# First sums of the up phase, their low parts and the norm steps rearranged in a Strassen feed-forward kernel

## The chip, the cores and the metric

The kernel runs on one core of one Trainium2 chip. The metric is the device time of one execution in microseconds (us); smaller is better. The core has a matrix engine (PE, TensorE), a vector engine (DVE, VectorE), a scalar engine (ACT, ScalarE), a general engine (POOL, GpSimd) and a queue (SP, SyncE) that here only starts transfers. POOL can start transfers too, and those can add what they carry to what stands at the destination ("accumulating transfer").

## The reference

One inference step of one encoder layer: 16 meta tokens and 1024 new frames of one stream, and 32 frames of a running stream, 1072 tokens of 1024 channels in all. A convolution group and an attention group run side by side; the change lies behind them, in the feed-forward part and the last norm:

```python
def rmsnorm(x, g):
    xf = x.astype(jnp.float32)
    r = lax.rsqrt(jnp.mean(xf * xf, axis=-1, keepdims=True) + EPS)
    return (xf * r).astype(x.dtype) * g

def conv_ffn(x, gate_past, g, w_up, dw_w, dw_b, w_down):
    h = rmsnorm(x, g)
    u = h @ w_up                                   # 1024 -> 2 x 2816
    gate, up = u[..., :D_FF], u[..., D_FF:]
    gate_ext = jnp.concatenate([gate_past, gate], axis=1)
    y = jax.nn.silu(depthwise_causal_conv(gate_ext, dw_w, dw_b)) * up   # width 3
    return x + y @ w_down, gate_ext[:, -(FFN_CONV_WIDTH - 1):]
...
    y_prompt = rmsnorm(xp, norm_final)[:, N_META:]
```

## The kernel before, in words

Channels lie on the 128 partitions, tokens along the rows. Every float32 product is made from three matmuls of a rounded format: each operand is split into a high part (a cast on ACT) and a low part (original minus high part), and the products high·high, high·low and low·high are summed (`mm3`). So each operand costs one cast and one subtraction. `hilo(hi, lo, raw)` does both, the subtraction on DVE or, with a fourth argument, on POOL (lines 1143 to 1145).

The feed-forward part is in two phases. **Up phase:** the 2816 channels are 22 blocks `f` of 128, each with a gate row `G` and an up row `Y`. Blocks 0 and 1 are multiplied plainly, in 16 groups of 24 matmuls (`group(f, u, p, c)`), blocks 2 to 21 by Strassen's method with 7 products instead of 8 (`up_strassen`). The activations' side of Strassen needs four sums of the four quarters b11, b12, b21, b22 of the input, times the norm's gain `g2`: b12-b11, b22-(b12-b11), b22-b12 and b21-(b22-(b12-b11)). These are the "first sums". `t_stage(p)` makes them for the two token halves `p`, in four steps `j` each, while PE works on the 16 plain groups: ACT scales the four quarters into `hraw`, DVE makes three sums into `traw` and the fourth into `t4`, ACT casts `traw` into the high parts `THI` and DVE subtracts for the low parts `TLO` (lines 1220 to 1236). The plain groups' weights go through two pairs of buffers (`plain`): `w_plain(1, 1)` overwrites the pair that block 0 used for `u` = 1. `rms2` gives the last third of the tokens its norm factors: sums by PE, a power on POOL, small steps on DVE, a diagonal on ACT, and a broadcast by PE (`last_rms`, lines 245 to 264). `gate_done` and `y_done` make a block's gate: multiply by the norm, convolution of width 3, silu, product.

**Down phase:** block rows come back from memory through three row buffers (`rb`, `gx`, `rbg`): `Feed.fill` issues a load on SP, `Feed.take` splits what has landed with `hilo` and frees the buffer for the next load. First 24 groups of plain products (`d_mm` over `arow`, line 1527), then eight Strassen steps (`STEPS`) whose results DVE adds to the residual rows `X` (line 1337), then the last four blocks plainly with the final norm (`rms_steps`, `final`). While the 24 groups run, `y_done(21)` stores the last block's row from the memory that the results of the last eight groups are copied to. `xd_add` adds the saved residual to `X` by accumulating transfers on POOL.

A scheduler decides the order on each engine where the program does not: PE's order is that of the program, ACT, DVE, POOL and SP are ordered by estimated readiness and priority, and each engine then runs its list strictly in order. Buffers are guarded by semaphores: whoever writes a buffer waits for its last reader.

Of the kernel before, what the change touches and what calls it, by code (L numbers as in the profile page):

```python
# [60 lines left out]
FS = 1  # L61
# [95 lines left out]
def body(nc, tc, cp, wp, xp, dp, io):  # L157
# [966 lines left out]
    traw = new(pr, "traw", 3 * PNS[0])  # L1124
    hraw = [new(pr, f"hraw{i}", 4 * PNS[0]) for i in range(2)]
# [3 lines left out]
    with tc.tile_pool(name="psB", bufs=1, space=PSUM, reuse_waits="tile") as pf:  # L1129
# [13 lines left out]
        def hilo(hi, lo, raw, eng=None):  # L1143
            nc.scalar.copy(hi, raw)  # L1144
            return (eng or nc.vector).tensor_tensor(out=lo, in0=raw, in1=hi.bitcast(F32), op=ALU.subtract)  # L1145
# [14 lines left out]

        def w_plain(f, u, hi, lo):
            raw = wraw(up_src(f, u))
            hilo(hi, lo, raw)
            ups[f, u] = kv(hi), kv(lo)
# [55 lines left out]
        def t_stage(p):  # L1220
            n = PNS[p]
            tt_ = nc.vector.tensor_tensor
            t4 = t4s[p][:, 0:4 * n].rearrange("p (a b) -> p a b", a=4)
            tr = traw[:, 0:3 * n].rearrange("p (a b) -> p a b", a=3)
# [146 lines left out]
        for i in range(4):  # L1371
            group(0, 0, i // 2, i % 2)
            if 0 < i < 3:
                next(last_rms)
            next(t0s)
        w_plain(1, 0, *plain[:2])
        for i in range(4):
            group(0, 1, i // 2, i % 2)
            if i == 1:
                next(last_rms)  # L1380
                gate_done(0)
            if i % 2:
# [36 lines left out]
        class Feed:  # L1419
# [59 lines left out]
        GQ = ((5, 1), (2, 0), (7, 1), (4, 0))  # L1479
# [230 lines left out]
```

## Time and profile before

| | |
|---|---|
| median of three runs | 1084.97 us (1083.0 to 1085.17) |
| the profiled execution | 1084.88 us |
| its span, first to last instruction | 1083.1 us |
| PE busy | 1046.9 us (97%) |
| DVE busy | 874.4 us (81%) |
| ACT busy | 499.5 us (46%) |
| POOL busy | 180.7 us (17%) |
| mean granted TensorE clock | 0.992 of full speed |

The profile is one execution. Times in it are us from the span's start. "PE 97% busy" is an average over stages, and a busy PE is not one at its peak, since matmuls overlap. What counts is where PE stands still, what ended that, and at which granted clock it goes on (1.00 is 2.4 GHz, 0.50 is 1.2 GHz). A time written as `a <-b` is idle time of an engine that ended when b was done.

### The profile page before, as it was taken

How to read it: one execution, taken by the hardware profiler on the slowest of the kernel's cores; microseconds unless marked ns; L12 is line 12 of the kernel's file. 1: busy time of each engine (PE TensorE's matmuls, PEld its weight loads, DVE VectorE, ACT ScalarE, POOL GpSimd, SP SyncE). 2: the span in 40 equal slices, each digit the busy share in tenths (PEclk: the TensorE clock that was granted, in tenths of full speed). 3: DMA queues.
4: the chain of work that ended last, by engine and by line, in shares of the span. 5: the costliest groups of instructions: out<-in, count | busy, mean ns of one | idle time of the engine just before them, and what ended most of it. 6: DMA issues, size and time to landing. Idle time of an engine off the chain costs nothing.

```text
span 1083.1 us, 19942 instructions
## 1 busy us (share of the span) xinstructions
PE 1046.9 (97%) x7741; PEld 1016.4 (94%) x7741; DVE 874.4 (81%) x1616; ACT 499.5 (46%) x1072; POOL 180.7 (17%) x199
## 2 busy tenths in 40 slices
PE   8999999989999989999999999999998999999995
PEld 7999997758999989999999999999998899999995
DVE  7799999999887788878888888888869766975645
ACT  8532226997776844333333433433336513522332
POOL 1112000002335121001001001000103330210042
PEclk9999999999999989999999999999999999999998
DMA  8344332124953122243242243233245794832214
GB/s 265 81 105 98 87 87 52 39 54 74 171 137 118 51 75 87 69 140 90 70 137 91 71 126 103 70 119 109 70 126 168 237 200 81 254 106 75 60 31 131
DMA packets 68119, 116.82 MB, mean 108 GB/s; under 512 B 11312, under 2 KB 44328, under 8 KB 68024
## 3 DMA queue, kind: packets, MB, share of 16 engines
q1 hardware_dynamic: 58200, 97.44, 28.7%
q0 software_dynamic: 9536, 17.89, 9.8%
q8 instruction: 61, 1.00, 0.4%
q14 instruction: 34, 0.28, 0.1%
q10 hardware_dynamic: 288, 0.22, 0.1%
HBM read 78.90 MB, written 27.51 MB: 98 GB/s over the span
## 4 chain that ended last, share of the span: by engine, by line
PE 55%; DVE 6%; DMA 3%; ACT 3%; issue 2%; POOL 1%; POOLq 0%; DVEq 0%; SPq 0%; ACTq 0%
PE mm L1209 49%; PE mm L241 2%; PE mm L239 2%; PE mm L240 2%; DMA raw<-wdn 1%; DVE bl L1145 1%; DMA gx<-yq 1%; DVE tl L1145 1%; DVE x L1262 1%; ACT hraw L1229 1%; DVE sl L1145 1%; DMA yd<-x 1%; DVE x L1582 1%; DVE gx L1256 0%; DVE wlo L1145 0%
## 5 line engine op out<-in xcount | busy, mean ns | idle before, releaser
L1209 PE MATMUL mm<-bh,sl 128*128 128x264 f32 (+1 forms) x912 | 214.7, 285 | 1.0 <-DVE x L1337 1.0
L365 DVE SCALAR_TENSOR_TENSOR acc<-glu,prm,acc 128x1090 f32<-128x1090 f32 (+3 forms) x180 | 168.0, 967 | 0.4
L1209 PEld LDWEIGHTS mm<-bh,sl 128*128 128x128 f32 x912 | 157.6, 189 | 1.2 <-DVE x L1337 1.2
L1209 PE MATMUL mm<-th,rawr 128*128 128x266 f32 (+1 forms) x640 | 121.3, 285 | 0.0
L1209 PE MATMUL mm<-bl,sl 128*128 128x264 f32 (+1 forms) x424 | 120.9, 285 | 0.0
L1209 PE MATMUL mm<-bh,wlo 128*128 128x264 f32 (+1 forms) x440 | 118.0, 285 | 0.0
L1209 PE MATMUL mm<-bh,whi 128*128 128x264 f32 (+1 forms) x440 | 113.1, 285 | 3.1 <-DVE x L1337 3.1
L1337 DVE TENSOR_TENSOR x<-x,mm 128x264 f32<-128x264 f32 (+7 forms) x238 | 75.8, 346 | 47.9 <-PE mm L1209 47.8
L239 PE MATMUL mm<-hi,whi 128*128 128x352 f32 (+3 forms) x312 | 104.8, 336 | 0.1
L240 PE MATMUL mm<-lo,whi 128*128 128x352 f32 (+3 forms) x312 | 102.3, 328 | 1.7 <-DVE lo L275 1.7
L241 PE MATMUL mm<-hi,wlo 128*128 128x352 f32 (+3 forms) x312 | 101.7, 326 | 0.0
L1209 PEld LDWEIGHTS mm<-th,rawr 128*128 128x128 f32 x640 | 101.2, 189 | 0.0
L1209 PE MATMUL mm<-th,sl 128*128 128x264 f32 (+1 forms) x352 | 93.1, 285 | 0.2 <-ACT th L1144 0.2
L1209 PE MATMUL mm<-tl,rawr 128*128 128x266 f32 (+1 forms) x320 | 91.4, 286 | 0.0
L1209 PEld LDWEIGHTS mm<-bh,whi 128*128 128x128 f32 x440 | 79.0, 189 | 3.5 <-issue 2.3
L1209 PEld LDWEIGHTS mm<-bh,wlo 128*128 128x128 f32 x440 | 80.7, 189 | 0.0
L1209 PEld LDWEIGHTS mm<-bl,sl 128*128 128x128 f32 x424 | 80.0, 189 | 0.0
L1209 PE MATMUL mm<-bl,whi 128*128 128x264 f32 (+1 forms) x272 | 77.4, 285 | 0.0
L1144 ACT CAST sl<-x 128x512 fp32r<-128x512 f32 (+1 forms) x41 | 29.7, 726 | 76.0 <-PE mm L1209 40.8
L1209 PEld LDWEIGHTS mm<-th,sl 128*128 128x128 f32 x352 | 64.2, 189 | 0.5 <-ACT th L1144 0.4
L240 PEld LDWEIGHTS mm<-lo,whi 128*128 128x128 f32 x312 | 59.2, 190 | 3.4 <-DVE lo L275 3.1
L239 PEld LDWEIGHTS mm<-hi,whi 128*128 128x128 f32 x312 | 59.1, 189 | 1.6 <-DVE acc L365 0.6
(350 smaller groups left out, 2941.0 us busy)
## 6 DMA issues: line engine op xcount, KB each, us to landing
x<-wup SPq DMA_DIRECT2D x40, 256.0 KB, 2.7
x<-wup SPq DMA_DIRECT2D x20, 512.0 KB, 4.3
yq<-x SPq DMA_DIRECT2D x32, 264.0 KB, 3.1
wlo<-raw POOLq DMA_DIRECT2D x16, 512.0 KB, 4.5
raw<-win SPq DMA_DIRECT2D x12, 512.0 KB, 3.5
raw<-wdn SPq DMA_DIRECT2D x12, 512.0 KB, 3.7
rb<-yq SPq DMA_DIRECT2D x10, 528.0 KB, 5.0
yq<-gx SPq DMA_DIRECT2D x16, 264.0 KB, 4.7
```

The source lines that it names most:

```text
L239: nc.tensor.matmul(ps, whi(k), xhi(k), start=first and i == 0, stop=False)
L240: nc.tensor.matmul(ps, whi(k), xlo(k), start=False, stop=False)
L241: nc.tensor.matmul(ps, wlo(k), xhi(k), start=False, stop=last and i == n - 1)
L365: nc.vector.scalar_tensor_tensor(out=a, in0=e[:, a0 + k:a1 + k], scalar=pcol("cw", p * CW + k), in1=a, op0=ALU.mult, op1=ALU.add)
L1144: nc.scalar.copy(hi, raw)
L1145: return (eng or nc.vector).tensor_tensor(out=lo, in0=raw, in1=hi.bitcast(F32), op=ALU.subtract)
L1209: nc.tensor.matmul(ps, w[:, j, :], x[:, j, :], start=first and j + i == 0, stop=j == 3 and i == 2, skip_group_check=True)
L1229: nc.scalar.activation(h[:, 2 * i * n + lo_:2 * i * n + hi_], src, AF.Copy, scale=pcol("g2", k))
L1262: nc.vector.scalar_tensor_tensor(out=Tm[:, NMETA:], in0=G[:, NMETA + k:k + GOW], scalar=pcol("fw", f * FW + k), in1=Tm[:, NMETA:], op0=ALU ...
L1337: nc.vector.tensor_tensor(out=z, in0=z, in1=banks[k][:, lo_:hi_], op=ALU.add)
L1582: nc.vector.scalar_tensor_tensor(out=x, in0=x, scalar=pcol("g3", k), in1=R[:, lo_:hi_], op0=ALU.mult, op1=ALU.mult)
```

## The change

There are four edits.

1. `t_stage` scales only one quarter (b11) on ACT; DVE takes the other three from `X` and applies the gain in the same instruction (`less`, a scalar_tensor_tensor). Where a quarter crosses from one residual tile into another, the instruction is made in two pieces. The third sum is now made as the second minus b11, the same value. `traw` becomes three buffers in turn, `hraw` shrinks.
2. The low parts `TLO` are made by `acc_lo`: ACT writes minus `raw`, rounded to the same format as the high part, and an accumulating transfer started by POOL adds `raw` to it, which leaves the rounding error, the low part.
3. The steps of `last_rms` and of the final norm (`fin`) are issued earlier: the former at high priority with its broadcast one group sooner, the latter ahead of the residual add of the same step. `w_plain(1, 1)` is issued ahead of the last step of `t_stage(1)` and of `y_done(0)`.
4. No `hilo` runs on POOL any more: the ten low parts that POOL made in the down phase go to DVE. The accumulating transfers of `xd_add` are no longer tied to the last of them; their row pairs come in the order 3, 0, 1 after the first Strassen step and 2 after the second, where it was 0, 1 and 3, 2.

```diff
-    traw = new(pr, "traw", 3 * PNS[0])
-    hraw = [new(pr, f"hraw{i}", 4 * PNS[0]) for i in range(2)]
+    traw = [new(pr, f"traw{i}", 3 * PNS[0]) for i in range(3)]
+    hraw = [new(pr, f"hraw{i}", PNS[0]) for i in range(2)]
...
+        def acc_lo(hi, lo, raw):
+            nc.scalar.copy(hi, raw)
+            nc.scalar.activation(lo, raw, AF.Copy, scale=-1.0)
+            nc.gpsimd.dma_start(lo, raw, accum_op=ALU.add)
...
+            def less(out, k, a, z):
+                for lo_, hi_, x in x_cols(k, a, n):
+                    nc.vector.scalar_tensor_tensor(out=out[:, lo_:hi_], in0=x, scalar=pcol("g2", k), in1=z[:, lo_:hi_],
+                                                   op0=ALU.mult, op1=ALU.subtract)
             for j in range(4):
-                h = hraw[j % 2]
-                for i, k in enumerate((j, 4 + j)):
-                    for lo_, hi_, src in x_cols(k, PAT[p], 2 * n):
-                        nc.scalar.activation(h[:, 2 * i * n + lo_:2 * i * n + hi_], src, AF.Copy, scale=pcol("g2", k))
-                b11, b12, b21, b22 = (h[:, i * n:i * n + n] for i in range(4))
-                tt_(out=tr[:, 0], in0=b12, in1=b11, op=ALU.subtract)
-                tt_(out=tr[:, 1], in0=b22, in1=tr[:, 0], op=ALU.subtract)
-                tt_(out=tr[:, 2], in0=b22, in1=b12, op=ALU.subtract)
-                tt_(out=t4[:, j], in0=b21, in1=tr[:, 1], op=ALU.subtract)
-                hilo(THI[p][:, :, j, :], TLO[p][:, :, j, :], tr)
+                h, tr = hraw[j % 2][:, :n], traw[j % 3][:, 0:3 * n].rearrange("p (a b) -> p a b", a=3)
+                hi, lo = THI[p][:, :, j, :], TLO[p][:, :, j, :]
+                for lo_, hi_, x in x_cols(j, PAT[p], n):
+                    nc.scalar.activation(h[:, lo_:hi_], x, AF.Copy, scale=pcol("g2", j))
+                less(tr[:, 0], j, PAT[p] + n, h)
+                less(tr[:, 1], 4 + j, PAT[p] + n, tr[:, 0])
+                nc.vector.tensor_tensor(out=tr[:, 2], in0=tr[:, 1], in1=h, op=ALU.subtract)
+                less(t4[:, j], 4 + j, PAT[p], tr[:, 1])
+                acc_lo(hi, lo, tr)
                 yield
...
             if 0 < i < 3:
-                next(last_rms)
+                with tc.high_priority():
+                    next(last_rms)
...
             group(0, 1, i // 2, i % 2)
+            if i == 0:
+                with tc.high_priority():
+                    next(last_rms)
+                gate_done(0)
             if i == 1:
-                next(last_rms)
-                gate_done(0)
-            if i % 2:
                 next(t1s)
+        w_plain(1, 1, *plain[2:])
+        next(t1s)
         y_done(0)
-        w_plain(1, 1, *plain[2:])
...
-        TAKES = {0: (None, None), 1: (nc.gpsimd,), 3: (nc.gpsimd,), 4: (None,), 9: (nc.gpsimd,), 12: (None,), 14: (nc.gpsimd,), 17: (None,), 18: (nc.gpsimd,)}
+        TAKES = {0: 2, 1: 1, 3: 1, 4: 1, 9: 1, 12: 1, 14: 1, 17: 1, 18: 1}
...
-                hook = lambda q, p: feed.take(nc.gpsimd if (q, p) in GQ else None)
+                hook = lambda q, p: feed.take()
...
-            for z in {0: (0, 1), 1: (3, 2)}.get(i, ()):
-                xd_add(z)
+            if i == 0:
+                with tc.issue_after(xd_add(3)):
+                    xd_add(0)
+                    xd_add(1)
+            if i == 1:
+                xd_add(2)
...
                 d_mm(ps, [z[:, m % 2] for z in wend[m // 2]], crow, t0, n)
+                if pos and m >= FS:
+                    next(fin, None)
                 if m == 0:
...
-                if pos and m >= FS:
-                    next(fin, None)
```

How the change moves instructions is seen at three places. First DVE, while PE works on the plain groups: the stretch that ends with the low part of the weights that `w_plain(1, 1)` loads (`wlo<-raw,whi`; `gx0` is the gate row, `x0` the row of the convolution, `traw`, `hraw` and `t4` belong to the first sums, `tl1` is a `TLO`). Before:

```order
L1256 TENSOR_TENSOR gx0_3621<-gx0_3621,rbg_3098 128x1060
L1232 TENSOR_TENSOR traw_3625<-hraw0_3626,traw_3625 128x264
L1259 TENSOR_SCALAR x0_2250<-gx0_3621,prm_66 128x1058
L1234 TENSOR_TENSOR t4_3628<-hraw0_3626,traw_3625 128x264
L1262 SCALAR_TENSOR_TENSOR x0_2250<-gx0_3621,prm_66,x0_2250 128x1058
L1145 TENSOR_TENSOR tl1_3620<-traw_3625,th1_3618 128x3x264
L1262 SCALAR_TENSOR_TENSOR x0_2250<-gx0_3621,prm_66,x0_2250 128x1058
L1145 TENSOR_TENSOR wlo_3638<-raw_3949,whi_3637 128x1024
```

And now:

```order
L1230 SCALAR_TENSOR_TENSOR traw0_3625<-x2_2252,prm_66,hraw1_3629 128x264
L1269 SCALAR_TENSOR_TENSOR x0_2250<-gx0_3621,prm_66,x0_2250 128x1058
L1230 SCALAR_TENSOR_TENSOR traw0_3625<-x2_2252,prm_66,traw0_3625 128x264
L1269 SCALAR_TENSOR_TENSOR x0_2250<-gx0_3621,prm_66,x0_2250 128x1058
L1240 TENSOR_TENSOR traw0_3625<-traw0_3625,hraw1_3629 128x264
L1230 SCALAR_TENSOR_TENSOR t4_3630<-x1_2251,prm_66,traw0_3625 128x176
L1230 SCALAR_TENSOR_TENSOR t4_3630<-x2_2252,prm_66,traw0_3625 128x88
L1145 TENSOR_TENSOR wlo_3640<-raw_3938,whi_3639 128x1024
```

The subtraction for `tl1` is gone from DVE, and the last step of the first sums (`hraw1`, on the first `traw` buffer) now stands ahead of the weights' low part, where it stood behind it.

Second DVE at the turn from the up to the down phase, from the last result added to the last block's gate row (`gx0<-gx0,mm`) on; `tl` and `bl` are low parts that the feed makes, `raw`, `sl` and `wlo` belong to the weights of the first Strassen step. Before:

```order
L1337 TENSOR_TENSOR gx0_3621<-gx0_3621,mm_8667 128x264
L1176 TENSOR_TENSOR raw_8617<-raw_8617 128x512
L1256 TENSOR_TENSOR gx0_3621<-gx0_3621,rbg_3098 128x1060
L1177 TENSOR_TENSOR raw_8617<-raw_8616,raw_8617 128x512
L1145 TENSOR_TENSOR sl_4085<-raw_8617,whi_3635 128x512
L1259 TENSOR_SCALAR x0_2250<-gx0_3621,prm_66 128x1058
L1145 TENSOR_TENSOR bl_3097<-x1_2251,bh_3096 128x4x264
L1182 TENSOR_TENSOR raw_8617<-raw_8617,raw_8616 128x512
L1262 SCALAR_TENSOR_TENSOR x0_2250<-gx0_3621,prm_66,x0_2250 128x1058
L1145 TENSOR_TENSOR wlo_3636<-raw_8617,sl_4085 128x512
```

And now:

```order
L1344 TENSOR_TENSOR gx0_3621<-gx0_3621,mm_8669 128x264
L1145 TENSOR_TENSOR tl0_3619<-rb_75,th0_3617 128x4x264
L1180 TENSOR_TENSOR raw_8619<-raw_8619 128x512
L1263 TENSOR_TENSOR gx0_3621<-gx0_3621,rbg_3098 128x1060
L1145 TENSOR_TENSOR tl1_3620<-x1_2251,th1_3618 128x1056
L1181 TENSOR_TENSOR raw_8619<-raw_8618,raw_8619 128x512
L1145 TENSOR_TENSOR bl_3097<-x1_2251,bh_3096 128x4x264
L1266 TENSOR_SCALAR x0_2250<-gx0_3621,prm_66 128x1058
L1145 TENSOR_TENSOR sl_4087<-raw_8619,whi_3637 128x512
L1145 TENSOR_TENSOR tl1_3620<-rb_75,th1_3618 128x1056
L1145 TENSOR_TENSOR wlo_3638<-raw_8619,sl_4087 128x512
L1269 SCALAR_TENSOR_TENSOR x0_2250<-gx0_3621,prm_66,x0_2250 128x1058
```

Three more low parts stand between the steps of the last block's gate.

Third ACT in the last stretch, where it squares the finished rows (into `rb`, `gx0`, `rbg`) and makes the diagonals of the norm of the 400 tokens before. Before:

```order
L1604 ACTIVATE rb_75<-x0_2250 128x256
L1604 ACTIVATE gx0_3621<-x0_2250 128x256
L1604 ACTIVATE rbg_3098<-x0_2250 128x256
L260 ACTIVATE diag0_93<-ident_67,stat_69 128x128
L260 ACTIVATE diag1_94<-ident_67,stat_69 128x128
L260 ACTIVATE diag2_95<-ident_67,stat_69 128x128
L260 ACTIVATE diag3_96<-ident_67,stat_69 128x128
```

And now:

```order
L1618 ACTIVATE rb_75<-x0_2250 128x256
L1618 ACTIVATE gx0_3621<-x0_2250 128x256
L260 ACTIVATE diag0_93<-ident_67,stat_69 128x128
L260 ACTIVATE diag1_94<-ident_67,stat_69 128x128
L260 ACTIVATE diag2_95<-ident_67,stat_69 128x128
L260 ACTIVATE diag3_96<-ident_67,stat_69 128x128
L1618 ACTIVATE rbg_3098<-x0_2250 128x256 x2
```

The diagonals come one square earlier; on POOL the power ahead of them comes one addition earlier.

## Rows read from the trace of the kernel before

**Rows 1.** The waits of PE over the whole span: what waited for what, us in total, times, longest.

```profile
PE mm L1209 <- DVE x L1337: 4.1, 3, 2.1
PE mm L239 <- ACT x L1527: 4.0, 5, 1.2
PE mm L241 <- DVE wlo L1145: 3.2, 1, 3.2
PE R L263 <- ACT diag L260: 2.9, 2, 2.1
```

**Rows 2.** Busy time by stretches of 2 us: width, then PE, PEld (weight load), DVE, ACT and POOL busy (instructions), granted clock, DMA share, GB/s.

```profile
383.00:385.00 2.00, 0.94 (x6) 0.51 (x4) 2.00 (x3) 0.92 (x2) 0.00 (x0) 1.00 0.00 0
385.00:387.00 2.00, 0.00 (x0) 0.00 (x0) 2.00 (x3) 0.72 (x1) 0.62 (x1) 0.68 0.00 0
387.00:389.00 2.00, 1.56 (x7) 1.57 (x8) 2.00 (x4) 0.97 (x4) 2.00 (x1) 0.50 0.00 0
```

**Rows 3.** The timeline of PE around the plain groups (start, us; in brackets the idle time before it): the norm's sums, its broadcast, and the first matmul of the first Strassen product.

```profile
358.02 0.83 PE L252 MATMUL R<-ones,rb 128*128 128x1 f32 x6 [0.27 <-POOL rb L271]
...
370.70 1.07 PE L263 MATMUL R<-diag,ones 128*128 128x128 f32 x6
...
407.26 0.28 PE L1209 MATMUL mm<-bh,sl 128*128 128x266 f32 x1
```

**Rows 4.** The timeline of DVE in the same stretch: two of the first sums, a low part of them, a step of the gate, the weights' low part.

```profile
379.51 0.43 DVE L1231 TENSOR_TENSOR traw<-hraw 128x264 f32<-128x264 f32 x1
379.86 0.42 DVE L1233 TENSOR_TENSOR traw<-hraw 128x264 f32<-128x264 f32 x1
...
384.04 0.97 DVE L1145 TENSOR_TENSOR tl<-traw,th 128x792 fp32r<-128x792 f32 x1
384.93 1.31 DVE L1262 SCALAR_TENSOR_TENSOR x<-gx,prm,x 128x1058 f32<-128x1058 f32 x1
386.17 1.22 DVE L1145 TENSOR_TENSOR wlo<-raw,whi 128x1024 fp32r<-128x1024 f32 x1
```

**Rows 5.** The timeline of ACT in the same stretch: the scaled quarters, a cast of the first sums, the cast of the weights.

```profile
353.26 3.36 ACT L1229 ACTIVATE hraw<-x,prm 128x324 f32<-128x324 f32 x8
...
381.84 0.85 ACT L1144 CAST th<-traw 128x792 fp32r<-128x792 f32 x1 [1.59 <-DVE traw L1232]
382.60 1.04 ACT L1144 CAST whi<-raw 128x1024 fp32r<-128x1024 f32 x1
```

**Rows 6.** The timeline of DVE in the last stretch: the last scaling by the norm.

```profile
1076.09 3.22 DVE L1582 SCALAR_TENSOR_TENSOR x<-x,prm,R 128x256 f32<-128x256 f32 x8 [1.68 <-PE R L263]
```

**Rows 7.** Transfers started by POOL, the list by issue: tiles, queue, times, KB each, median us from issue to landing. `wlo<-raw` and `cal<-ca` accumulate within the core's own memory, as the new transfers do; `x<-xd` is `xd_add`, which accumulates from the main memory.

```profile
wlo<-raw POOLq DMA_DIRECT2D x16, 512.0 KB, 4.5
...
x<-xd POOLq DMA_DIRECT2D x4, 384.0 KB, 11.2
...
cal<-ca POOLq DMA_DIRECT2D x1, 384.0 KB, 4.4
```

**Rows 8.** The view of line 229, the issues of `wlo<-raw` on POOL: shortest, median and longest in ns, first and last start.

```profile
L229 POOL DMA_DIRECT2D wlo<-raw x15: 839/845/1389, 32.8 to 279.2; - x15
```

**Rows 9.** The timeline of POOL at the turn to the down phase.

```profile
820.36 2.69 POOL L1145 TENSOR_TENSOR tl<-rb,th 128x1056 fp32r<-128x1056 f32 x1 [21.30 <-ACT th L1144]
823.02 2.92 POOL L1145 TENSOR_TENSOR tl<-x,th 128x1056 fp32r<-128x1056 f32 x1
...
829.76 3.36 POOL L1145 TENSOR_TENSOR tl<-rb,th 128x1056 fp32r<-128x1056 f32 x1 [0.49 <-ACT th L1144]
```

**Rows 10.** The timeline of DVE in the same stretch.

```profile
821.17 2.43 DVE L1176 TENSOR_TENSOR raw<-raw 128x512 f32<-128x512 f32 x1
823.52 3.54 DVE L1256 TENSOR_TENSOR gx<-gx,rbg 128x1060 f32<-128x1060 f32 x1
826.98 0.68 DVE L1177 TENSOR_TENSOR raw<-raw 128x512 f32<-128x512 f32 x1
...
830.70 3.53 DVE L1262 SCALAR_TENSOR_TENSOR x<-gx,prm,x 128x1058 f32<-128x1058 f32 x1
```

**Rows 11.** The chain of waits in order of time from 842 on (start, us, what).

```profile
842.26 6.11 DMA yd<-x
...
848.48 0.43 ACT x L1527
```

**Rows 12.** The timeline of DVE in the fourth Strassen step and behind it: three low parts.

```profile
924.91 2.83 DVE L1145 TENSOR_TENSOR sl<-raw,wlo 128x1024 fp32r<-128x1024 f32 x1
...
934.22 2.46 DVE L1145 TENSOR_TENSOR bl<-gx,bh 128x1056 fp32r<-128x1056 f32 x1 [0.44 <-ACT bh L1144]
...
949.23 2.55 DVE L1145 TENSOR_TENSOR sl<-raw,wlo 128x512 fp32r<-128x512 f32 x1
```

**Rows 13.** The timeline of PE there: the two matmuls that waited longest.

```profile
930.98 0.39 PE L1209 MATMUL mm<-bh,sl 128*128 128x264 f32 x1 [1.00 <-DVE x L1337]
...
953.91 0.36 PE L1209 MATMUL mm<-bh,whi 128*128 128x264 f32 x1 [2.08 <-DVE x L1337]
```

**Rows 14.** The timeline of PE in the last stretch.

```profile
1063.21 1.36 PE L263 MATMUL R<-diag,ones 128*128 128x128 f32 x8 [0.81 <-ACT diag L260]
```

**Rows 15.** The timeline of POOL there: the addition ahead of the power, and the power.

```profile
1059.71 0.74 POOL L1606 TENSOR_TENSOR rb<-rb,gx 128x256 f32<-128x256 f32 x1 [1.43 <-ACT gx L1604]
1060.41 1.02 POOL L254 TENSOR_TENSOR stat<-stat,mhalf 128x4 f32<-128x4 f32 x1
```

More of the change, by code (lines that the diff above doesn't have):

```diff
@@ L1141, in body, with hilo @@
         free = []
-        def hilo(hi, lo, raw, eng=None):
+        def hilo(hi, lo, raw):
             nc.scalar.copy(hi, raw)
-            return (eng or nc.vector).tensor_tensor(out=lo, in0=raw, in1=hi.bitcast(F32), op=ALU.subtract)
+            nc.vector.tensor_tensor(out=lo, in0=raw, in1=hi.bitcast(F32), op=ALU.subtract)
         def kv(z):
@@ L1159, in body @@
         ups = {}
+        def acc_lo(hi, lo, raw):
+            nc.scalar.copy(hi, raw)
+            nc.scalar.activation(lo, raw, AF.Copy, scale=-1.0)
+            nc.gpsimd.dma_start(lo, raw, accum_op=ALU.add)
         def w_plain(f, u, hi, lo):
-            raw = wraw(up_src(f, u))
-            hilo(hi, lo, raw)
+            hilo(hi, lo, wraw(up_src(f, u)))
             ups[f, u] = kv(hi), kv(lo)
@@ L1221, in t_stage @@
             n = PNS[p]
-            tt_ = nc.vector.tensor_tensor
             t4 = t4s[p][:, 0:4 * n].rearrange("p (a b) -> p a b", a=4)
-            tr = traw[:, 0:3 * n].rearrange("p (a b) -> p a b", a=3)
+            def less(out, k, a, z):
+                for lo_, hi_, x in x_cols(k, a, n):
+                    nc.vector.scalar_tensor_tensor(out=out[:, lo_:hi_], in0=x, scalar=pcol("g2", k), in1=z[:, lo_:hi_],
+                                                   op0=ALU.mult, op1=ALU.subtract)
             for j in range(4):
-                h = hraw[j % 2]
-                for i, k in enumerate((j, 4 + j)):
-                    for lo_, hi_, src in x_cols(k, PAT[p], 2 * n):
-                        nc.scalar.activation(h[:, 2 * i * n + lo_:2 * i * n + hi_], src, AF.Copy, scale=pcol("g2", k))
-                b11, b12, b21, b22 = (h[:, i * n:i * n + n] for i in range(4))
-                tt_(out=tr[:, 0], in0=b12, in1=b11, op=ALU.subtract)
-                tt_(out=tr[:, 1], in0=b22, in1=tr[:, 0], op=ALU.subtract)
-                tt_(out=tr[:, 2], in0=b22, in1=b12, op=ALU.subtract)
-                tt_(out=t4[:, j], in0=b21, in1=tr[:, 1], op=ALU.subtract)
-                hilo(THI[p][:, :, j, :], TLO[p][:, :, j, :], tr)
+                h, tr = hraw[j % 2][:, :n], traw[j % 3][:, 0:3 * n].rearrange("p (a b) -> p a b", a=3)
[7 more added lines that the diff above has]
+                acc_lo(hi, lo, tr)
                 yield
@@ L1430, in fill, with take @@
                     self.ready.append((dst, raw, z))
-            def take(self, eng=None, keep=True):
+            def take(self, keep=True):
                 dst, raw, z = self.ready.pop(0)
-                self.last = hilo(*dst, raw, eng).ins
+                hilo(*dst, raw)
                 if keep:
@@ L1477, in run @@
                 pass
-        GQ = ((5, 1), (2, 0), (7, 1), (4, 0))
         STEPS = [(c, mp) for c in range(2) for mp in (3, 2, 1, 0)]
@@ L1515, in body @@
         run(up_strassen(NF - 1, [(q, p) for q in SEQL for p in range(2)]), None, first_hook)
-        TAKES = {0: (None, None), 1: (nc.gpsimd,), 3: (nc.gpsimd,), 4: (None,), 9: (nc.gpsimd,), 12: (None,), 14: (nc.gpsimd,), 17: (None,), 18: (nc.gpsimd,)}
+        TAKES = {0: 2, 1: 1, 3: 1, 4: 1, 9: 1, 12: 1, 14: 1, 17: 1, 18: 1}
         for i, (m, b) in enumerate([(m, b) for m in range(KD - 1, -1, -1) for b in (1, 2)] +
                                    [(m, 0) for m in range(KD - 1, -1, -1)]):
-            for e in TAKES.get(i, ()):
-                feed.take(e, i >= 9)
+            for _ in range(TAKES.get(i, 0)):
+                feed.take(keep=i >= 9)
                 if i == 3:
@@ L1530, in body @@
         feed = Feed([f_job(0, q, p) for q in (7, 3) for p in range(2)], late)
-        for e in (None, None, None, nc.gpsimd):
-            feed.take(e)
-        mark = feed.last
+        for _ in range(4):
+            feed.take()
         def xd_add(mp):
-            with tc.issue_after(mark):
-                for b, (t0, n) in enumerate(YB):
-                    nc.gpsimd.dma_start(X[b][:, 2 * mp:2 * mp + 2, t0 - OB[b][0]:],
+            for b, (t0, n) in enumerate(YB):
+                z = nc.gpsimd.dma_start(X[b][:, 2 * mp:2 * mp + 2, t0 - OB[b][0]:],
                                         xd[:, 2 * mp:2 * mp + 2, t0 - H0:t0 - H0 + n], accum_op=ALU.add)
+            return z.ins
         wend = []
```

## The prediction

> **What bounds the kernel now.** I read the page first: PE is busy for 97% of the span, so no other engine bounds the kernel on average, and a gain can only come from places where PE stands still or runs at half clock. The waits of PE name them [rows 1]. Four touch the change: 3.2 us at once on the weights' low part `wlo`, 4.1 in three waits on DVE's L1337, 4.0 in five on ACT's L1527, and 2.9 in two on the norm's diagonal.
>
> The 3.2 us cost more than 3.2. By the stretches [rows 2], PE all but stops within 383 to 385, does nothing from 385 to 387, and the granted clock goes from 1.00 through 0.68 to 0.50 (1.2 GHz) when it resumes. How much that is comes from the timeline of PE [rows 3]: between the norm's sums (358.02, 0.83 long) and its broadcast (370.70, 1.07 long) lie four groups, so a group takes (370.70 - 358.02 - 0.83) / 4 = 2.96 us. Ten groups behind the broadcast should end at 370.70 + 1.07 + 29.6 = 401.4; the first Strassen product starts at 407.26. So 5.9 us are lost: 3.2 of wait and some 2.7 of clock. With the 0.27 ahead of the norm's sums [rows 3], at most 6.1 (rounded down) can come back.
>
> The wait itself is a queue on DVE [rows 4]. `wlo` starts at 386.17 because it stands behind a `tl` (0.97), two convolution steps L1262 (1.31 each) and first sums that wait for ACT. Its cast was done by 382.60 + 1.04 [rows 5].
>
> **Up phase, what changes.** Three `hraw` scalings of a step leave ACT (3.36 / 8 = 0.42 each [rows 5]) and a negation as long as a cast, 0.85 [rows 5], comes; ACT has room. DVE keeps four or so small instructions a step, 0.35 apart [rows 4]; the form with a gain is bounded by the final norm's, 3.22 / 8 = 0.40 [rows 6]. It loses the 0.97 of `tl` in each of eight steps.
>
> What comes instead is the landing of a 409 KB accumulating transfer (128 x 792 x 4 bytes). No such transfer of first sums exists before. Nearest are those within the core's own memory: 4.5 us for 512 KB and 4.4 for 384 KB [rows 7]; the farthest is `x<-xd`, 11.2 us for 384 KB from the main memory, nine issued together. I take 4.4, issue included (0.845 of POOL, 1.389 at worst [rows 8], on an otherwise idle POOL).
>
> A `traw` buffer is free again only when its transfer has landed. Buffer 0 is used three times before the step that now stands ahead of `wlo`: steps 0 and 3 of the first half, step 0 of the second. That makes a new chain. A use takes sums 1.5, cast 0.85, negation 0.85 and landing 4.4, so 7.6. The first begins at the scaling at 353.26 [rows 5]: 353.26 + 0.42 + 7.6 = 361.3, and 2 us for what ACT does between, an estimate, make 363.3. The next two land at 370.9 and 378.5. Then DVE does the last step's pieces with two L1262 between, 3 x 0.35 + 2 x 1.31 + 0.4 = 4.1, and `wlo` 1.22: done at 383.8.
>
> PE comes for it when? The broadcast now stands one group sooner: reached at 358.0 + 0.83 + 3 x 2.96 = 367.7 less the 0.27, ended at 368.5, and five groups on it is 383.3. So PE waits 0.5; with some hand-overs between engines I take 0.7, too short for the fall of the clock seen behind the 3.2. Gain 6.1 - 0.7 = 5.4. Each us more per landing puts 3 us on that wait. Bounds from these rows: 6.1 without a wait; 2.6 with a wait like today's but shorter by a landing's spread.
>
> The Trainium skill, DMA: Bandwidth & Descriptors, section "Anatomy of one DMA — SWDGE (gpsimd) path", gives a transfer started by POOL some 2.0 us plus its bytes at 436 KB per us: an estimate of 2.9 us here. The trace differs: 4.4 to 4.5 from the issue's start [rows 7]. By the page each landing is 1.5 us shorter, PE would not wait, and the sum below would be 1075.3.
>
> **Turn to the down phase.** Three low parts move from POOL to DVE, each 1.22 there (a length as of `wlo` [rows 4]): 3.7 more. Against it: while POOL ran them for 2.69, 2.92 and 3.36 [rows 9], DVE's instructions beside them took 2.43, 3.54 and 3.53 [rows 10], where the like take 0.68 [rows 10], about 1.25 (as L1262 and `wlo`) and 1.31 [rows 4]. That stretch is (2.43 - 0.68) + (3.54 - 1.25) + (3.53 - 1.31) = 6.3, and it goes. So the last block's gate ends 6.3 - 3.7 = 2.6 earlier, less about 0.8 because the third low part must wait for a row that is loaded again: 1.8. Behind the gate stands the store `yd<-x`, 6.11, and behind it ACT's copy L1527 [rows 11], which is what PE waits for in five places, 4.0 in all [rows 1]. I take 1.8 of it; bounds 0 (PE then waits for the feed instead) and 4.0.
>
> **Strassen steps.** Likewise at 924, 934 and 949 three low parts on DVE took 2.83, 2.46 and 2.55 [rows 12], with 1.22 and, for the half-size one, 0.68 as their like: 1.6, 1.2 and 1.9 of stretch, against one more low part of 1.22 on DVE for each. Little is left over: 1.0 of the two waits of 1.00 and 2.08 [rows 13] is my value, bounds 0 and 3.1. DVE is the busiest engine there, so nothing hides the three if the stretch has another cause. The transfers of `xd_add` now start behind the first Strassen step's last addition; the rows are wanted two steps later, some 40 us against 11.2 [rows 7]: nothing.
>
> **Tail.** The power on POOL comes one addition (0.74) earlier [rows 15], the diagonals one square earlier, and PE waits 0.81 for the first of them [rows 14]: 0.8 goes (bounds 0 and 1.0, the power itself being 1.02 [rows 15]). The last norm's wait of 2.1 [rows 1] stays, with the scaling behind it [rows 6].
>
> **Sum.** 5.4 + 1.8 + 1.0 + 0.8 = 9.0. The profiled execution took 1084.88, 1.78 of it outside its span of 1083.1, and lies 0.09 below the median of 1084.97. So 1084.97 - 9.0 = 1076.0. All upper bounds, 14.2, give 1070.8; all lower, 2.6, give 1082.4.
>
> **Rivals.**
> *The wait changes its name.* The landings take 5.5 instead of 4.4 (1.389 per issue [rows 8] explains half of that), `wlo` is 3.3 late and the clock falls once more: up phase 6.1 - 4.0 - 2.5, near nothing. Or the low parts on DVE eat what POOL's absence gives. The former leaves 3.2 us, the latter 5.4 + 0.8: 1081.8 or 1078.8, about 1080. For: three landings in series where none was. Against: the two nearest rows agree within 0.1.
> *The gain is given back.* The forms of the first Strassen step follow PE's plain groups, and if the high and low parts of t are not there 6 us sooner, the wait moves to the first product: about 1082.
> *Slower.* One mechanism: the landings behave like `x<-xd`, because three transfers are under way at once. The break-even: three times the excess x over 4.4, plus 2.5 of clock, against 6.1 + 3.6, so x = 2.4, a landing of 6.8; at 7.8 the time is 1085 + 3 = 1088, at 11.2 it is 1098. For: 11.2 stands in the same queue [rows 7]. Against: those nine come together from the main memory, and the DMA share around the stall is 0.00 [rows 2].
> *The edit doesn't do what it says:* the order of DVE shows `wlo` behind all of the last step; if DVE blocks there on the landing, the first edit has only moved the queue. That is the first rival's price.
>
> **Chances.** Forecast 0.62, first rival 0.24, second 0.07, slower 0.06, and 0.01 for less than the forecast's bounds. About 0.2% (2.2 us) is what this kernel's measurement can tell. Faster takes the forecast, the first rival but for a little, and most of the second: 0.88; same 0.06; slower 0.06. The likeliest case alone ranges over 1072 to 1079; with the first rival and most of the second the range is 1071.5 to 1082.
>
> **What would show it.** In the new profile: the wait of PE on `wlo` L1145 near 383 is gone or under 1 us, and no stretch from 383 to 392 is at 0.50; the first Strassen product starts near 401.5; DVE waits for transfers ahead of the fourth step of each half; the transfers of `traw` land in 4 to 5 us; at the turn DVE's L1263 and L1269 take 1.25 to 1.3 and the wait on L1527's copy totals about 2; the wait of 0.81 in the tail is gone. I am wrong if PE waits over 2 us on `wlo` or at the first product, if the clock falls there again, if the turn's waits grow, or if the long DVE instructions at the turn stay long without POOL.

## The result and the profile after

The changed kernel took 1077.55 us (median of 6 runs, 1076.28 to 1078.31) against 1084.2 for the kernel before (6 runs, 1082.06 to 1085.17): a ratio of 0.994, 95% interval 0.9927 to 0.9953, so 6.6 us faster. The forecast was 1076.0 with a range of 1071.5 to 1082. The total is near it, but the terms it was summed from are not: the largest had the wrong sign, so that the total is near is luck.

To see that, the same matmuls are looked up in both traces and their starts compared (us). What the last column loses or gains from one line to the next was lost or gained between them:

| matmul of PE | before | after | shift |
|---|---|---|---|
| the norm's sums, first row of [rows 3] | 358.02 | 357.11 | -0.91 |
| first Strassen product, last row of [rows 3] | 407.26 | 408.49 | +1.23 |
| behind a wait ahead of the turn | 813.39 | 813.80 | +0.41 |
| last wait of the turn | 848.95 | 845.35 | -3.60 |
| second row of [rows 13] | 953.91 | 948.49 | -5.42 |
| the tail's broadcast [rows 14] | 1063.21 | 1056.84 | -6.37 |
| end of the span | 1083.1 | 1076.3 | -6.8 |

Half of the -0.91 (0.48) stands there at 342 already, ahead of the change. So from 342 to the first Strassen product this trace lost 1.7 us, where a gain of 5.4 was forecast, and everything behind it gained 8.0, where 3.6 was forecast.

One pair of traces does not fix the 1.7. From the norm's sums at 342 to the first product it is 64.6 before and 66.3 after; it is 63.7 in run 1 below, which has the up phase of before, and 65.3 to 65.7 in runs 5, 6, 10 and 11, which have that of the changed kernel. Each trace of the new up phase is longer than both of the old one, by 0.7 to 2.7, on average by some 1.5. The sign is shown, the size only roughly.

The waits of PE after the change, which answer to [rows 1] (what waited for what, us in total, times, longest):

```profile
PE R L263 <- ACT diag L260: 4.3, 2, 2.2
PE mm L241 <- DVE wlo L1145: 3.1, 1, 3.1
PE mm L1213 <- DVE x L1344: 1.7, 3, 1.2
PE mm L239 <- ACT x L1536: 1.7, 1, 1.7
```

The wait on `wlo` is still there, 3.1 instead of 3.2, and the norm's diagonal costs a new wait of 2.2 (the other of its two is the tail's 2.1, as before); what shrank are the two others, both of the down phase. The three that are left there answer to [rows 11, 13]:

```profile
845.35 0.41 PE L239 MATMUL mm<-th,bh 128*128 128x320 f32 x1 [1.70 <-ACT x L1536]
927.98 0.39 PE L1213 MATMUL mm<-bh,sl 128*128 128x264 f32 x1 [0.36 <-DVE x L1344]
948.49 0.36 PE L1213 MATMUL mm<-bh,whi 128*128 128x264 f32 x1 [1.19 <-DVE x L1344]
```

The timeline of PE in the up phase and the busy time by stretches (width, PE, PEld, DVE, ACT, POOL, granted clock, DMA share, GB/s), which answer to [rows 2, 3]:

```profile
357.11 0.72 PE L252 MATMUL R<-ones,rb 128*128 128x1 f32 x6
368.90 1.52 PE L263 MATMUL R<-diag,ones 128*128 128x128 f32 x6 [2.18 <-ACT diag L260]
389.41 0.46 PE L241 MATMUL mm<-bh,wlo 128*128 128x264 f32 x1 [3.10 <-DVE wlo L1145]
408.49 0.28 PE L1213 MATMUL mm<-bh,sl 128*128 128x266 f32 x1
```

```profile
368.00:378.00 10.00, 9.10 (x62) 9.10 (x63) 6.28 (x15) 8.33 (x21) 3.61 (x4) 0.83 0.69 99
370.00:372.00 2.00, 2.00 (x11) 2.00 (x11) 0.61 (x3) 1.89 (x4) 0.00 (x0) 0.50 1.07 156
387.00:389.00 2.00, 0.00 (x0) 0.00 (x0) 2.00 (x5) 1.62 (x2) 0.25 (x1) 1.00 0.00 0
389.00:391.00 2.00, 1.59 (x8) 1.59 (x9) 1.97 (x3) 1.57 (x5) 0.74 (x1) 0.65 0.42 135
391.00:393.00 2.00, 2.00 (x11) 2.00 (x11) 0.89 (x2) 0.00 (x0) 0.52 (x1) 0.50 0.52 78
```

The clock falls twice now, to 0.50 behind either wait (a mean of 0.83 from 368 to 378). DVE shows why PE waits (answers to [rows 4]):

```profile
364.39 0.63 DVE L1230 SCALAR_TENSOR_TENSOR traw<-x,prm,hraw 128x58 f32<-128x58 f32 x2 [3.14 <-DMA tl<-traw]
366.23 0.15 DVE L253 TENSOR_SCALAR stat<-R 128x3 f32<-128x3 f32 x1
373.07 0.49 DVE L1230 SCALAR_TENSOR_TENSOR traw<-x,prm,hraw 128x264 f32<-128x264 f32 x1 [2.46 <-DMA tl<-traw]
383.98 0.49 DVE L1230 SCALAR_TENSOR_TENSOR traw<-x,prm,hraw 128x264 f32<-128x264 f32 x1 [3.32 <-DMA tl<-traw]
388.14 1.22 DVE L1145 TENSOR_TENSOR wlo<-raw,whi 128x1024 fp32r<-128x1024 f32 x1
```

Three times DVE stands idle until a transfer has landed in the chain that the prediction drew: 364.4, 373.1 and 384.0, where it had 363.3, 370.9 and 378.5. Behind the first stands the norm's step L253, whose sums PE had ready at 358; behind the third stands `wlo`. The view of line 1164, the issues on POOL (shortest, median, longest in ns), and how long each took to land (answers to [rows 7, 8]):

```profile
L1164 POOL DMA_DIRECT2D tl<-traw x8: 1258/1278/1300, 359.5 to 390.3; - x8
DMA to landing us min/median/max: 4.7/5.0/7.0
```

The 7.0 is that of the issue at 376.95, for which DVE waits until 383.98; the two that DVE waits for before it take 4.8 each.

At the turn the stretched instructions of [rows 10] are gone: DVE's L1180, L1263 and L1269 (L1176, L1256 and L1262 before) take 0.68, 1.25 and 1.31.

```profile
822.85 0.68 DVE L1180 TENSOR_TENSOR raw<-raw 128x512 f32<-128x512 f32 x1
823.46 1.25 DVE L1263 TENSOR_TENSOR gx<-gx,rbg 128x1060 f32<-128x1060 f32 x1
...
830.69 1.31 DVE L1269 SCALAR_TENSOR_TENSOR x<-gx,prm,x 128x1058 f32<-128x1058 f32 x1
```

The wait of 1.70 that is left at the turn has another end than the one of [rows 11]. There it was the store `yd<-x`; now, by the chain of waits, it is the load `rbg<-yq`, whose cast stands ahead of the copy L1536 in ACT's queue:

```profile
837.65 6.22 DMA rbg<-yq
...
844.88 0.43 ACT x L1536
```

### The profile page after: what moved, and what is told of

It is laid out like the page before. It is cut to its first block, busy times and chain, and to the rows that moved or that the text cites. A ratio compares the mean times of both kernels' runs of the same rounds, so it can differ in the third digit from the quotient of the medians.

```text
span 1076.3 us, 19947 instructions
## 1 busy us (share of the span) xinstructions
PE 1045.0 (97%) x7741; PEld 1016.9 (94%) x7741; DVE 868.7 (81%) x1630; ACT 496.2 (46%) x1060; POOL 165.9 (15%) x197
## 4 chain that ended last, share of the span: by engine, by line
PE 77%; DVE 9%; DMA 5%; ACT 4%; issue 3%; POOL 0%; SPq 0%; POOLq 0%; DVEq 0%; ACTq 0%
PE mm L1213 49%; PE mm L239 8%; PE mm L241 8%; PE mm L240 8%; DVE acc L365 2%; DMA tl<-traw 2%; DMA rbg<-yq 1%; DMA rb<-yq 1%; ACT pb L696 1%; DVE tl L1145 1%; DVE x L1594 1%; DVE x L1344 1%; PE R L263 1%; DVE bl L1145 1%; DVE pb L689 1%
## 5 line engine op out<-in xcount | busy, mean ns | idle before, releaser
L1213 PEld LDWEIGHTS mm<-tl,rawr 128*128 128x128 f32 x320 | 60.4, 189 | 0.0
```

What stands on the lines that cost most here:

```text
L1213: nc.tensor.matmul(ps, w[:, j, :], x[:, j, :], start=first and j + i == 0, stop=j == 3 and i == 2, skip_group_check=True)
```

## The experiments

Each is an edit of the changed kernel. Ratios are to the kernel before, on the same chip and in the same session; the changed kernel's is 0.994 (0.9927 to 0.9953). Its own time was taken in an earlier session, and the kernel before took 1084.2 to 1085.5 from session to session, so it is the ratios that compare. "Start" is that of the first Strassen product in the trace (408.49 in the changed kernel, 407.26 before).

| run | median us | ratio, 95% interval | start |
|---|---|---|---|
| 1 e1_up_before | 1076.19 | 0.9923, 0.9907 to 0.9940 | 406.16 |
| 2 e2_lo_dve | 1072.48 | 0.9887, 0.9872 to 0.9901 | 403.23 |
| 3 e3_bcast_old | 1076.96 | 0.9927, 0.9911 to 0.9944 | 409.62 |
| 4 e4_wlo_first | 1074.96 | 0.9905, 0.9887 to 0.9922 | 404.23 |
| 5 e5_pool_turn | 1081.96 | 0.9970, 0.9957 to 0.9982 | 407.45 |
| 6 e6_pool_steps | 1081.47 | 0.9959, 0.9944 to 0.9974 | 407.73 |
| 7 e7_flat | 1078.23 | 0.9934, 0.9919 to 0.9949 | 409.70 |
| 8 e8_best | 1070.73 | 0.9866, 0.9850 to 0.9881 | 399.58 |
| 9 e9_light_loads | 1075.93 | 0.9921, 0.9904 to 0.9937 | 407.92 |
| 10 e10_tail_old | 1078.29 | 0.9942, 0.9930 to 0.9955 | 407.98 |
| 11 e11_xd_old | 1086.21 | 1.0015, 1.0002 to 1.0029 | 407.50 |
| 12 e12_best_acc | 1071.28 | 0.9872, 0.9846 to 0.9898 | 400.44 |

### 1: the up phase as before

`t_stage`, its buffers and the order of the plain groups are those of the kernel before.

> The changed kernel with the whole up phase (first sums, low parts, the places of the norm steps and of the weights' load) put back as it was before; the down phase and the tail stay changed. Theory: the up phase as changed loses 2.2 us (the first Strassen product starts 1.23 later, and PE had come 0.91 sooner to the norm's sums), and the whole gain lies behind it. Then the product starts near 407, the wait of 1.0 at 813 comes back, and the time is 1076.3 (1075.3 to 1077.3), under the changed kernel's 1077.55. Rival: the up phase gains something that the records hide, and without it the time goes to 1080 or more.

Measured 1076.19; the product starts at 406.16, 2.3 sooner than in the changed kernel's trace and 1.3 to 1.8 sooner than in the four other traces with its up phase (runs 5, 6, 10 and 11). The traces bear the theory out: with the up phase of before PE is there earlier. The wait ahead of the turn, 0.75 instead of 0.19, says little, for it is 0.44 to 0.80 in those four too. In the medians the difference is 1.4, less than the intervals tell apart. The rival, 1080 or more, is out: the gain lies behind the up phase.

### 2: low parts on DVE

```diff
-                acc_lo(hi, lo, tr)
+                hilo(hi, lo, tr)
```

> The changed kernel with one edit undone: the low parts of the first sums are subtracted on DVE again, with no transfer. Theory (the landing is the cause): DVE's three waits on transfers, 8.9 us, go, and 8 subtractions of 0.97 come; the norm's diagonal comes about 1.3 us sooner, so PE waits under 1 for it instead of 2.18 and the clock stays; the wait on wlo stays at 2 to 3 because wlo still stands at the end of DVE's queue. Time 1074.5 (1073 to 1076). Rival (the new order alone makes the waits): both waits stay within 0.5 us and the time is 1077.5.

Measured 1072.48, just below the range forecast, and with the two waits the other way round: the one on `wlo` is gone, which was to stay. DVE does eight more subtractions and still reaches `wlo` 5.2 us sooner. But PE waits for the diagonal nearly as long as in the changed kernel, where under 1 was forecast, and the clock is 0.50 from 370 to 372 here too:

```profile
382.92 1.21 DVE L1145 TENSOR_TENSOR wlo<-raw,whi 128x1024 fp32r<-128x1024 f32 x1
368.50 1.07 PE L263 MATMUL R<-diag,ones 128*128 128x128 f32 x6 [1.76 <-ACT diag L260]
```

So the landing makes the second wait; the first has another cause (L253 runs at 364.72 here, with its sums ready at 358, still behind the first sums in DVE's queue).

### 3: the broadcast in its old place

```diff
-            if i == 0:
-                with tc.high_priority():
-                    next(last_rms)
-                gate_done(0)
             if i == 1:
+                next(last_rms)
+                gate_done(0)
                 next(t1s)
```

> The changed kernel with the norm's broadcast and its step back in their old places, one group later. Theory (the landing is the cause): the wait of 2.18 and the fall of the clock behind it go, but PE only comes sooner to wlo, which the third landing in a row on one buffer sets; the wait there grows from 3.1 to about 6 and the time stays, 1077.5 (1076 to 1078.5). Rival (the order is the cause): wlo moves with PE, 1074.

Measured 1076.96, as the theory has it. PE does not wait for the diagonal, and waits 6.35 on `wlo` instead of 3.10:

```profile
PE mm L241 <- DVE wlo L1145: 6.4, 1, 6.4
```

The first wait is in effect hidden by the second: removing it alone gained nothing here.

### 4: `wlo` ahead of the last step

```diff
-            if i in (0, 2):
+            if i == 0:
                 next(t1s)
+            if i == 2:
+                with tc.issue_after(last_w):
+                    next(t1s)
```

> The changed kernel with one thing moved: the last step of the first sums is issued behind the weights' low part wlo, so DVE does not stand before the third landing with wlo behind it. Theory (the landing, met through the queue): PE's wait of 3.1 on wlo falls under 0.5 and the clock does not fall there; 1073.5 (1072.5 to 1075). Rival one (wlo is late for its own reasons: DVE's convolution steps): wait 2 or more, 1077. Rival two (the last step is now late for the first Strassen step's weights, whose loads overwrite what it reads): PE waits at the first product instead, 1077 or more.

Measured 1074.96, 1.5 over the forecast but inside its range. `wlo` starts at 385.42 (388.14 in the changed kernel), PE waits 0.71 for it and the clock stays at 1.00 behind that wait; the product starts 4.3 sooner than in the changed kernel's trace, 3.2 to 3.8 sooner than in the four others with its up phase. The longest landing still takes 6.2, so it is its place in the queue that costs.

```profile
385.42 1.22 DVE L1145 TENSOR_TENSOR wlo<-raw,whi 128x1024 fp32r<-128x1024 f32 x1
386.69 0.39 PE L241 MATMUL mm<-bh,wlo 128*128 128x264 f32 x1 [0.71 <-DVE wlo L1145]
```

### 5 and 6: POOL's low parts back

```diff
-                feed.take(keep=i >= 9)
+                feed.take(keep=i >= 9, eng=nc.gpsimd if i in (1, 3, 9) else None)
```

> The changed kernel with the three low parts at the turn to the down phase made on POOL again, nothing else. Theory (POOL's instruction stretches DVE's beside it): three or four of DVE's instructions there take 2.4 to 3.6 again, the gate of the last block ends 2.6 later, PE's waits behind the store come to 3 to 4 again instead of 1.7, and the time is 1080 (1079 to 1081.5). Rival (the turn gained because the up phase came later, or through the order on DVE): long instructions or not, the time stays within 1 of 1077.55.

> The changed kernel with the four low parts of the fourth Strassen step made on POOL again, nothing else. Theory (the same stretch): DVE's instructions near 920 to 950 take 2.5 to 2.8 again and the two waits of PE there come back from 0.4 and 1.2 to 1.0 and 2.1; 1079 (1078 to 1080). Rival (these waits shrank because the accumulating transfers of xd_add start at another time): both waits stay, 1077.5.

Run 5 measured 0.997, a loss of 3.3 against 0.994, and the two intervals do not meet; its median of 1081.96 is 0.5 above the range forecast. DVE's two longest at the turn:

```profile
823.19 3.52 DVE L1263 TENSOR_TENSOR gx<-gx,rbg 128x1060 f32<-128x1060 f32 x1
830.36 3.53 DVE L1269 SCALAR_TENSOR_TENSOR x<-gx,prm,x 128x1058 f32<-128x1058 f32 x1
```

They are the 3.54 and 3.53 of [rows 10] within 0.02, while three 1.25 us low parts have left DVE. PE's waits for L1536 come to 4.5 in five places again, and against the changed kernel its matmuls go from 0.44 early at 813 to 3.84 late behind the last of these waits. Run 6, the same in the fourth Strassen step, measured 0.9959, 2.1 slower than 0.994; here the intervals overlap, and the median of 1081.47 is 1.5 above the range forecast. What it shows, its trace shows: three of DVE's low parts take 2.82, 2.53 and 2.71 again, and the waits of [rows 13] are back, where the changed kernel has 0.36 and 1.19:

```profile
925.78 0.39 PE L1213 MATMUL mm<-bh,sl 128*128 128x264 f32 x1 [0.93 <-DVE x L1344]
948.62 0.37 PE L1213 MATMUL mm<-bh,whi 128*128 128x264 f32 x1 [1.97 <-DVE x L1344]
```

Both rivals fall. What stretches DVE's instruction, one with two operands in the core's own memory, is an instruction of POOL beside it that reads that memory: with POOL's low parts back the stretch is back, without them it is gone. The Trainium skill, SBUF — State Buffer, section "Who interferes with whom", says that a vector instruction with two inputs there contends with a POOL instruction that reads there, over a port that the two share and that is locked, not divided. The rows agree: the L1256 of [rows 10] ends at 827.06, 1.1 behind the low part on POOL that runs from 823.02 to 825.94 [rows 9], so nearly all of its 1.25 comes after it. It goes in the other direction as well: in the changed kernel it is POOL that stands, while DVE runs three such instructions in a row (1.25, 0.68 and 1.25), and POOL's copy of two elements takes 2.92 where the same line took 0.33:

```profile
379.10 0.33 POOL L1264 COPY stout<-gx 128x2 f32<-128x2 f32 x1
...
824.77 2.92 POOL L1264 COPY stout<-gx 128x2 f32<-128x2 f32 x1 [24.49 <-DVE gx L1263]
```

### 7: another form of the same transfer

```diff
-                hi, lo = THI[p][:, :, j, :], TLO[p][:, :, j, :]
+                hi = THI[p][:, :, j, :]
+                lo = flat(TLO[p].rearrange("p a b c -> p (a b) c"))[:, 3 * j * n:3 * j * n + 3 * n].rearrange("p (a b) -> p a b", a=3)
```

> The changed kernel with the transfers of the first sums writing one whole stretch per partition (3.2 KB) instead of three rows of 1.06 KB; the low parts so land in other places, and the products that use them get wrong numbers, at the same cost. Theory (the form of the transfer makes it slow): an issue takes 0.85 instead of 1.28 on POOL and a landing 4.4 instead of 5.0, as the older transfers do; wlo comes 1.5 sooner; 1076 (1075 to 1077). Rival (the size and what runs beside it set the landing): issue and landing stay, 1077.5.

```profile
L1164 POOL DMA_DIRECT2D tl<-traw x8: 844/854/912, 359.7 to 390.3; - x8
DMA to landing us min/median/max: 4.0/4.4/7.7
```

Issue and median landing are as the theory has them, 0.854 and 4.4. The time is not: 1078.23, above its range. The landing that decides, the third on buffer 0, took 7.7 here, and the scheduler put the cast `whi` behind a step of the gate that waits for it too: PE waited 4.29 on `whi` and 0.72 on `wlo`. So the form sets the issue and the usual landing, but not the long one, and it is the long one that PE waits for.

### 8: both queues put right

Three moves on top of run 2: the third and fourth step of the first half behind the norm's last step; the gate of block 0 and the last step of the first sums behind `wlo`.

```diff
+            if i < 2:
+                next(t0s)
+            else:
+                with tc.issue_after(norm_end[-1]):
+                    next(t0s)
...
+        last_w = w_plain(1, 1, *plain[2:])
+        with tc.issue_after(last_w):
+            gate_done(0)
```

> A version built from the runs so far: low parts of the first sums on DVE as in e2_lo_dve; the third and fourth step of the first half issued behind the last step of the norm, so that the norm's power does not wait in DVE's queue; the gate of block 0 and the last step of the first sums issued behind the weights' low part wlo. Theory (both remaining waits of the up phase are places in DVE's queue): PE waits under 0.5 for the norm's diagonal and for wlo, the clock stays at 1.00, the first Strassen product starts near 401, and the time is 1069.5 (1068.5 to 1071). Rival: what is moved back is late for the first Strassen product, PE waits there, 1072 or more.

Measured 1070.73, where before ran at 1085.48: ratio 0.9866, which is 14.5 us faster than before and 8 faster than the changed kernel. PE waits for neither the diagonal nor `wlo`:

```profile
366.59 0.83 PE L265 MATMUL R<-diag,ones 128*128 128x128 f32 x6
```

The clock is 1.00 from 364 to 402, PE is busy all through it, and the product starts at 399.58, even sooner than the 401.4 that the prediction's groups gave for no wait.

### 9: lighter loads beside the late landing

```diff
-                nc.sync.dma_start(z, y)
+                nc.sync.dma_start(z[:, few], y[:, few])
```

> The changed kernel with the three weight loads of the first Strassen block (1 MB in all, started by SP from 376 on) cut to a sixteenth of their bytes, so that block's products get wrong weights at the same cost. Theory (the longest landing, 7.0 where the others take 5.0, shares the DMA engines with these loads): that landing falls to about 5, DVE's wait there from 3.3 to 1.3, PE's wait on wlo from 3.1 to 1.1, and the clock stays; 1074.5 (1073.5 to 1076). Rival (it is long through POOL or DVE, which work beside its issue): 7.0 stays and the time is 1077.5.

Inconclusive. The landing took 6.0 and PE's wait on `wlo` was 2.25, between the two. But runs with full loads show 6.1 to 7.0 for the same landing (6.1 in run 5, 6.3 in run 6, 6.4 in run 10), and run 5 with full loads has a wait of 2.14. At most 1 us is the loads'; what else makes it longer than the median of 5.0 stays open. POOL's copy of two elements right behind its issue took 1.33, beside a long instruction of DVE, where the next such copy took 0.25; but the issue itself took 1.28, as all do, and in run 7 that copy took 0.18 and the landing 7.7. Whether DVE holds the transfer up after its issue was not tried.

### 10: the tail as before

```diff
-                if pos and m >= FS:
-                    next(fin, None)
...
+                if pos and m >= FS:
+                    next(fin, None)
```

> The changed kernel with the steps of the final norm behind the residual add again, as before. Theory: PE's wait of 0.8 for the diagonal near 1057 comes back and the time is 0.7 longer, 1078.2 (1077.5 to 1079). Rival (the tail's gain is made by what comes before it): the wait stays away, 1077.5.

The wait is back, 0.82 at 1057.33, and there PE falls back by 0.7 against the changed kernel. The median, 1078.29, is where the theory puts it; the ratio, 0.9942, can't be told from 0.994.

### 11: `xd_add` tied as before

```diff
-            if i == 0:
-                with tc.issue_after(xd_add(3)):
-                    xd_add(0)
-                    xd_add(1)
-            if i == 1:
-                xd_add(2)
+            for z in {0: (0, 1), 1: (3, 2)}.get(i, ()):
+                xd_add(z)
```

> The changed kernel with the accumulating transfers of xd_add tied and ordered as before. Theory (only POOL's low parts matter in the Strassen steps): PE's waits in the fourth step stay at 0.4 and 1.2 or less, and the time stays, 1077.5 (1076.5 to 1078.5). Rival (the transfers' times share in the gain of the fourth step): the waits grow to 1.0 and 2.1, 1079.

Measured 1.0015, some 8 us slower than the changed kernel: neither theory nor rival. The waits in the fourth step stay small (0.36 and 0.43), as the theory has it; the loss is at the turn. The tie was to the last low part; that one is DVE's now, and does not hold POOL back. POOL starts the transfers as soon as their rows are written:

```profile
832.59 1.19 POOL L1547 DMA_DIRECT2D x<-xd  x1 [1.94 <-DMA rb<-yq]
837.04 2.40 POOL L1547 DMA_DIRECT2D x<-xd  x2 [1.43 <-ACT x L1536]
```

Before it was 863, in the changed kernel 866.61. Here they lie beside the loads and the store of the turn (DMA share 1.11 from 840 to 850, 0.88 in the changed kernel). The chain of waits shows what that costs: the store `yd<-x`, 6.11 in [rows 11], takes 13.45, and behind it ACT's copy L1536, for which PE waits 5.3 in all, with the clock at 0.70 from 850 to 860.

```profile
838.29 13.45 DMA yd<-x
...
851.82 0.43 ACT x L1536
```

So the new tie and order of `xd_add` are no ornament: without them, the removal of POOL's low parts would have been given back in full. Which of the two does it, this run does not separate.

### 12: the best version with transfers

Run 8 with `acc_lo` in place of `hilo`.

> The version e8_best with one difference: the low parts of the first sums are made by the accumulating transfers again. Theory (the landings cost only through what stands behind them in DVE's queue, and here neither the norm's steps nor wlo stands behind the late one): DVE still waits some 8 us for landings, PE waits for neither the diagonal nor wlo, and the time is that of e8_best within 1 us, a ratio to before of 0.9865 to 0.988. Rival (three landings in a row cost the path wherever they stand): PE waits 2 us or more at wlo, at the next group's results or at the first Strassen product, ratio 0.990 or more.

Ratio 0.9872, which can't be told from run 8's 0.9866. PE waits 1.0 on `wlo`, which the theory did not have, and not for the diagonal; the product starts 0.9 later than in run 8. DVE stands before landings 4.3 us in all, less than expected, and the late one is still there (2.16 at 386.17, longest landing 6.4). It costs PE little, since neither the norm's steps nor `wlo` stands behind it in DVE's queue.

## Why the prediction was right in the total and wrong in its largest term

**What bounds the kernel.** Right: `wlo` in DVE's queue and the clock behind it. Run 8 removes both and starts the first product 7.7 sooner than before (7.2, counted from 342 on), more than the 6.1 that the prediction allowed.

**Up phase: wrong.** Two steps failed. The first is "I take 4.4, issue included": the issue takes 1.28, not 0.845, the landings 5.0 (median), and the one that counts 7.0 (6.1 to 6.4 in runs 5, 6, 10 and 11). The 512 KB row it came from writes one stretch per partition; the new transfer writes three, and run 7 shows that this makes the difference of 0.4 in the issue and, with medians of 4.8 to 5.0 in the changed form, 0.4 to 0.6 in the landing. With ACT's and POOL's steps between, a round of the buffer took 8.7 and 10.9 instead of 7.6. So `wlo` was done 5.6 late: 2.6 of it is the one landing of 7.0, whose cause stays open (runs 7 and 9), the rest the steps between and the other two landings. The prediction had said that each us of landing puts 3 on `wlo`; it is the first rival that came true here, "the wait changes its name", except that the wait kept even its name. The Trainium skill, DMA: Bandwidth & Descriptors, section "Anatomy of one DMA — SWDGE (gpsimd) path", has a fit that for these bytes gives an estimate of 2.9; no run has less than 4.0, so the measurement decides against it. The size in the prediction is a slip without weight: 128 x 792 x 4 bytes are 406 KB, not 409.

The second is "the broadcast now stands one group sooner: reached at 367.7": PE was there at 366.7, but the diagonal was not. The prediction checked when PE would come, not when L253, L255 and L257 would pass DVE; they stand behind first sums, be it with transfers (L253 at 366.23) or without (run 2, 364.72). In the changed kernel that cost a wait of 2.18 and a fall of the clock; it did not show in the total, since `wlo` was later still (run 3).

**Turn: right in mechanism, too small.** The sum had 2.6 less 0.8, and took 1.8 of a bound of 4.0; measured 4.0 over the turn by the shifts, 3.3 by the ratios (run 5). What was mis-sized is the subtraction of 0.8 for a row that is loaded again: the trace shows the three low parts on DVE without such a wait. Nor was 4.0 a bound: PE's waits shrank by 2.3, from 4.0 to 1.7, while the shift came to 4.0. Of the 0.7 to 1.4 beyond 2.6 the runs show no single cause.

**Strassen steps: right, and nearer the upper bound.** 1.8 by the shifts, 2.1 by run 6, for 1.0. "Little is left over" counted DVE's time as one sum. A low part that moves into an idle stretch of DVE should cost nothing, and a stretch ahead of a wait all of it; that is argued, no run tried it.

**`xd_add`: nothing, as it stands.** But for a reason that the prediction did not see (run 11).

**Tail: right**, 0.8 forecast, 0.7 in the trace (run 10).

So the sum of 9.0 came out at 6.6 because a term of +5.4 turned to a loss of some 1.5 (1.7 in this trace, with 0.8 given back at the wait ahead of the turn), and terms of 2.8 in the down phase were 5.8. That the two errors nearly cancel is luck. Of the prediction's own signs of being wrong two came true: PE waits over 2 us on `wlo`, and the clock falls there again.

## What to carry to other kernels

A transfer that replaces an instruction frees an engine and adds a latency; ask for each buffer that it guards what stands behind the next writer in that engine's strictly ordered queue, and move that ahead before judging the transfer (runs 4 and 12). A step that is issued earlier is only earlier if every engine on its chain lets it pass. A transfer tied to an instruction is tied to its engine: when that instruction moves, look where the transfer goes.

## What the runs showed of the hardware that was not expected

- The same 399 KB, written in one stretch per partition or in three: 0.854 or 1.278 us of POOL for the issue, 4.4 or 4.8 to 5.0 to the landing (medians; run 7, and the changed kernel with runs 5, 6, 10 and 11).
- The length of a wait alone does not tell whether the clock falls behind it. The wait of 2.18 that ends at 368.90 is followed by 0.50 from 370 to 372, and so is that of 2.13 in run 5 and even that of 1.76 in run 2; at the same place 2.13 in run 6 and 2.15 in run 11 are followed by 1.00. The 2.08 of [rows 13] is followed by 1.00 from 953 to 960, and the 1.97 of run 6, at the same matmul, by 0.50 from 950 to 952.
- DVE and POOL stretch each other: 3.54 instead of 1.25 for DVE's L1256, 2.92 instead of 0.33 for a copy of two elements on POOL.
- A store took twice its time beside other transfers: `yd<-x` 6.11 before and 13.45 in run 11, where four of the transfers of `xd_add` were issued from 832 to 839.
